# HGRN's values in a hybrid HGRN2 + RWKV-7 layer: turned by VectorE in 32x32 blocks and small transfers, where TensorE transposes did it

## The chip, the core and the metric

The kernel runs on one core of a Trainium2 chip. The metric is the time of one execution on the device in microseconds (us), and a version's time is the median of several runs. Engines are named as in the profile: PE is TensorE's matmul, PEld its weight load, DVE is VectorE, ACT is ScalarE, POOL is GpSimd, SP is SyncE, which here only issues transfers. Every engine works through its own instructions in a fixed order; an instruction that waits holds up all behind it.

## The reference, cut to what matters

One decoder layer over 2048 tokens of width 1024. A normalised input is projected once; four heads of HGRN2 and eight heads of RWKV-7 take their columns, their outputs are projected back, and a ConvFFN follows. The value `v` of this study is `i_raw`, of width 512, four heads of 128.

```python
h = _rmsnorm(x, norm1_w[l]);  proj = h @ w_in[l]
q_raw, f_raw, i_raw, g_raw = jnp.split(hg_p, 4, axis=-1)
...
f = lb + (1.0 - lb) * jax.nn.sigmoid(f_raw)
q = heads(jax.nn.silu(q_raw)) * (HG_HEAD_DIM ** -0.5);  k = heads(1.0 - f);  v = heads(i_raw)
# chunkwise: o_t = S_t^T q_t,  S_t = diag(f_t) S_{t-1} + k_t v_t^T
A = jnp.einsum('bhtk,bhsk,bhtsk->bhts', qb, kb, dec)
o = jnp.einsum('bhts,bhsv->bhtv', A, vb) + jnp.einsum('bhtk,bhkv->bhtv', qb * jnp.exp(b), S)
S = jnp.exp(b_last[:, :, 0, :])[..., None] * S + jnp.einsum('bhsk,bhsv->bhkv', kb * jnp.exp(b_last - b), vb)
```

The input projection yields `v` with channels on the 128 partitions and tokens along the row. The sums over `s` (tokens) on TensorE want tokens on the partitions: `v` has to be turned.

## The kernel before

The program has two stages. Stage one (`phase1`, up to about 1303 us) makes the projection, both mixers and most of the output projection; stage two the ConvFFN. The 2048 tokens are four blocks (`nb`) of 512. Stage one weaves three streams of work together:

- `dense`: per block 30 column groups of 128 (`P` jobs). Each is 24 matmuls `pj` (lines 270 to 272: high and low halves of inputs `hh`, `hl` and weights `wh`, `wl`) into one of two `pj` banks, and then an evacuation function takes the bank: `ev_rkv` and its kin for RWKV-7, `ev_q`, `ev_f`, `ev_v`, `ev_g` for HGRN. The four of HGRN's head `j` follow each other in this order. Between the blocks lie the transposes of the next input (`turn`), those of a finished block (job `N`: `transposed` with `to_h2`, tiles `h`, stored to `h2d`), and the output projection `out_block` (job `O`), which loads the mixers' output in tiles `oraw`.
- `rw_super`, eight times: RWKV-7 for a block and two pairs of heads. VectorE makes `M` (line 733) and block-turns `KB` to `KBb` (line 754); SP sends `KBb` on to `KBT` in 16 transfers (line 757), `M` to DRAM as `Ed` in four (line 745) and back as `E` in two (line 748). On `E`, VectorE runs a chain of 62 small steps (`etmp`, `Ti`, lines 802 and 804), then `TZ`, and PE goes on at line 821.
- `hg_unit`, 16 times: HGRN for a block and one head. Its first step turns `v`: four TensorE transposes (line 952) of the SBUF tile `hv` into a bank `hg`, and an ACT copy to `VT`. Then come scaled queries and keys `hX`, their matmuls (line 990), the turned keys `KT`, the products `KT` x `VT` (line 1055, the first user of `VT`) and `Af` x `VT` (line 1064).

Each round of the loop at the end of `phase1` takes one step (up to a `yield`) of `rw_super`, one of `hg_unit`, and 2000 ns by an estimate of `dense`. A scheduler then orders the instructions of each engine by its own model of their durations, so a change in one place moves others. Tiles named with a tag and `bufs=2` share two buffers in turn: tag `sg` holds the sigmoids `sgm` of `ev_q` and `ev_g` and, in `out_block`, `oraw`. SP's queue holds nearly all transfers but the weights, which POOL issues.

Of the kernel before, what the change touches and what calls it, by code (L numbers as in the profile page):

```python
# [7 lines left out]
F32 = mybir.dt.float32  # L8
# [3 lines left out]
AF = mybir.ActivationFunctionType  # L12
# [6 lines left out]
P = 128  # L19
# [48 lines left out]
def tile_layer(ctx, tc, consts, x, norm1_w, w_in, hg_lb_logits, hg_norm_w, rw_shift_mu, rw_w0, rw_w2,  # L68
# [4 lines left out]
    V, S, TE = nc.vector, nc.scalar, nc.tensor  # L73
    dma, store = nc.sync.dma_start, nc.gpsimd.dma_start
# [11 lines left out]
    ident = cp.tile([P, P], F32, name="ident")  # L86
# [27 lines left out]
    def act(out_, in_, func, **kw):  # L114

        want = tables.get(func)
        if want is not None and want != tab["now"]:
            pre = S.preload_act_table_set(want)
            for u_ in tab["uses"]:
                tc.add_manual_dep(pre.ins, u_.ins.name, NOSYNC, reason="table order")  # L120
            tab.update(now=want, pre=pre, uses=[])
        i_ = S.activation(out_, in_, func, **kw)  # L122
        if want is not None:
            tc.add_manual_dep(i_.ins, tab["pre"].ins.name, NOSYNC, reason="table order")
            tab["uses"].append(i_)
        return i_
# [119 lines left out]
    def split_to(hi, lo, src):  # L246
        c_ = S.copy(hi, src)
        return c_, V.tensor_sub(lo, src, hi.bitcast(F32))
# [25 lines left out]
    def phase1(c1):  # L274
# [3 lines left out]
        rp = c1.enter_context(tc.tile_pool(name="rp", bufs=1, reuse_waits="tile"))  # L278
# [18 lines left out]
        def bank(kind):  # L297
            return ps.tile([P, 512], F32, tag=kind, name=kind, bufs=2)
# [4 lines left out]
        stage = {}  # L303


        def stg(tag, name, bufs):
            return sp.tile([P, BLK], F32, tag=tag, name=name, bufs=bufs)
# [49 lines left out]

        def ev_v(nb, j):
            def f(acc):
                t_ = stg("hv", "hv", 2)  # L360
                act(t_, acc, AF.Copy)
                stage[("v", nb, j)] = t_
            return f

# [577 lines left out]


        def hg_unit(nb, j):
            q, f, v, gg = (stage.pop((n_, nb, j)) for n_ in "qfvg")
            k = rp.tile([P, BLK], F32, tag="hk", name="hk")
            V.tensor_scalar(k, f, -1.0, 1.0, ALU.mult, ALU.add)

            VT = rp.tile([P, 4, P], F32, tag="VT", name="VT")
            tp = bank("hg")  # L950
            for b in range(4):
                TE.transpose(tp[:, b * P:(b + 1) * P], v[:, b * P:(b + 1) * P], ident)
            act(VT, tp.rearrange("p (b t) -> p b t", t=P), AF.Copy)
            yield
            A = rp.tile([P, 4, 32], F32, tag="hA", name="A")
            Pf = f
            Sf = rp.tile([P, BLK], F32, tag="Sf", name="Sf")
# [83 lines left out]
            tp = bank("hg")  # L1041
# [12 lines left out]
            for b in range(4):  # L1054
                TE.matmul(sps[:, b * P:(b + 1) * P], KT[:, b, :], VT[:, b, :], start=True, stop=True)
            for b in range(4):
# [5 lines left out]
            for b in range(4):  # L1062
                ts_ = slice(b * P, (b + 1) * P)
                TE.matmul(op[:, ts_], VT[:, b, :], Af[:, b, :], start=True, stop=False)
                TE.matmul(op[:, ts_], SH[:, b, :], q[:, ts_], start=False, stop=True)
            sq = rp.tile([P, BLK], F32, tag="hk", name="osq")
            act(sq, op, AF.Square)
            hi, lo = (rp.tile([P, BLK], F32R, tag=tag, name="part") for tag in ("Sf", "VT"))
            split_to(hi, lo, sq)
# [22 lines left out]
        def hg_stream():  # L1092
            for n in range(4 * NBLK):
                while ready["hg"] <= n:
                    yield None
                yield from hg_unit(n // 4, n % 4)
# [47 lines left out]
    with ExitStack() as c2:  # L1144
# [36 lines left out]
        with tc.tile_pool(name="op", bufs=1, reuse_waits="tile") as op_:  # L1181
# [7 lines left out]
            b = NBLK - 1  # L1189
# [53 lines left out]
            for dh in range(2):  # L1243
                accs = [pst("wacc") for _ in range(4)]
                for n, k in enumerate((0, 1, 4, 5, 2, 3, 6, 7)):
# [16 lines left out]
                    if dh == 1 and 2 <= n:  # L1262
                        for j in range(2):
                            q = 2 * (n - 2) + j
# [3 lines left out]
                    for q in range(12):  # L1268
                        i, t_ = (q % 4, q // 4) if first else (q // 3, q % 3)
# [231 lines left out]
    with tc.tile_pool(name="dn", bufs=1, reuse_waits="tile") as dn:  # L1501
# [61 lines left out]
        for s_ in range(DS, N):  # L1563
            g, p, kk = steps[s_]
# [4 lines left out]
            acc = accs[DP[p][0]]  # L1569
# [55 lines left out]
```

## Time and profile before

| what | value |
|---|---|
| median of 3 runs | 2646.53 us (2640.78 to 2649.34) |
| the profiled execution, its own time | 2645.42 us |
| its span, first to last instruction | 2643.6 us |
| granted PE clock, mean | 0.994 |
| ACT copies `hv` and `VT` | 16 each, median 598 ns each |
| TensorE transposes of `hv` | 64 |
| transfers `KBb` to `KBT` | 128 of 64 KB |

The profile is of one execution. A row of a group gives how often an instruction ran, its busy time and the mean of one, then the idle time of its engine just before it and what ended it. Matmuls are pipelined, so that one starts before the last has ended: what one costs on PE is the distance from its start to the next one's, not its duration.

### The profile page before, as it was taken

Reading aid. Unit: us, or ns where it says so; the run is one execution under the profiler, and the core shown is the slowest. Engines: PE = TensorE matmul, PEld = TensorE weight load, DVE = VectorE, ACT = ScalarE, POOL = GpSimd, SP = SyncE. Lnnn points to the kernel's source line nnn. Section 1 sums busy time; section 2 is a strip of 40 time slices with the busy share of each in tenths; the row PEclk is TensorE's granted clock in tenths of the full one; section 3 lists DMA queues with packets and bytes.
Section 4 is the critical chain, followed back from the end, with each engine's and each line's share of the span. In section 5 each row is a group of like instructions: output and inputs, shape, how many; then the busy total and the mean of one; then the engine's idle time right before and its main releaser. Section 6 shows DMA issues by size and latency. Waiting matters only on the chain.

```text
span 2643.6 us, 51054 instructions
## 1 busy us (share of the span) xinstructions
PE 2547.0 (96%) x19467; PEld 2046.8 (77%) x19467; DVE 1963.7 (74%) x3744; ACT 1372.7 (52%) x2258; POOL 382.1 (14%) x686
## 2 busy tenths in 40 slices
PE   7999999999999999899899999999999999999998
PEld 5877777777777767777678888887888887888887
DVE  4868677676576765777678789988988887766556
ACT  5555444555545555344466654556554544545444
POOL 6433222212222122232100000000000000000000
PEclk9999999999999999999999999999999999999999
DMA  8846463555655565845583467747763553998655
GB/s 304 239 147 195 152 168 116 143 159 205 190 173 138 174 212 179 261 151 150 181 287 124 136 221 257 240 154 232 245 203 129 171 171 128 334 321 283 200 191 187
DMA packets 380298, 518.98 MB, mean 196 GB/s; under 512 B 114463, under 2 KB 211093, under 8 KB 380053
## 3 DMA queue, kind: packets, MB, share of 16 engines
q1 hardware_dynamic: 325521, 337.38, 40.1%
q0 software_dynamic: 54464, 178.32, 20.9%
q8 instruction: 153, 2.51, 0.4%
q14 instruction: 92, 0.75, 0.1%
q10 hardware_dynamic: 68, 0.02, 0.0%
HBM read 372.99 MB, written 134.22 MB: 192 GB/s over the span
## 4 chain that ended last, share of the span: by engine, by line
PE 70%; DVE 11%; ACT 8%; DMA 7%; issue 3%; POOL 0%; SPq 0%; DVEq 0%; ACTq 0%; POOLq 0%
PE pj L270 7%; PE pj L271 7%; PE pj L272 6%; PE ua L270 5%; PE ua L272 5%; PE ua L271 5%; PE da L271 3%; PE da L272 3%; PE da L270 3%; PE ud L271 2%; PE ud L270 2%; PE ud L272 2%; PE db L272 2%; PE db L271 2%; PE db L270 2%
## 5 line engine op out<-in xcount | busy, mean ns | idle before, releaser
L270 PE MATMUL pj<-hh,wh 128*128 128x512 f32 x960 | 391.6, 408 | 6.1 <-ACT rkv L122 4.0
L271 PE MATMUL pj<-hl,wh 128*128 128x512 f32 x960 | 377.4, 393 | 0.0
L272 PE MATMUL pj<-hh,wl 128*128 128x512 f32 x960 | 377.4, 393 | 0.0
L270 PE MATMUL ua<-Bh,uwh 128*128 128x512 f32 x704 | 276.4, 393 | 3.5 <-ACT m L122 2.2
L272 PE MATMUL ua<-Bh,uwl 128*128 128x512 f32 x704 | 274.3, 390 | 0.0
L271 PE MATMUL ua<-Bl,uwh 128*128 128x512 f32 x704 | 274.1, 389 | 0.0
L270 PEld LDWEIGHTS pj<-hh,wh 128*128 128x128 f32 x960 | 180.9, 189 | 54.5 <-issue 7.0
L272 PEld LDWEIGHTS pj<-hh,wl 128*128 128x128 f32 x960 | 180.8, 188 | 39.4 <-DMA wl<-Win171l 0.3
L271 PEld LDWEIGHTS pj<-hl,wh 128*128 128x128 f32 x960 | 181.0, 189 | 35.0 <-DVE hl L488 0.5
L254 ACT CAST uwh<-uraw 128x512 fp32r<-128x512 f32 x220 | 134.3, 617 | 135.0 <-PE ua L271 55.7
L255 DVE TENSOR_TENSOR dal<-draw,dah 128x512 fp32r<-128x512 f32 x138 | 95.2, 690 | 108.3 <-ACT dah L254 105.7
L255 DVE TENSOR_TENSOR uwl<-uraw,uwh 128x512 fp32r<-128x512 f32 x220 | 147.1, 684 | 34.3 <-ACT uwh L254 34.3
L254 ACT CAST dah<-draw 128x512 fp32r<-128x512 f32 x138 | 85.8, 621 | 160.0 <-PE da L271 75.5
L270 PEld LDWEIGHTS ua<-Bh,uwh 128*128 128x128 f32 x704 | 132.2, 188 | 33.9 <-ACT m L122 5.6
L272 PEld LDWEIGHTS ua<-Bh,uwl 128*128 128x128 f32 x704 | 132.2, 188 | 28.1 <-DVE uwl L255 0.4
L271 PEld LDWEIGHTS ua<-Bl,uwh 128*128 128x128 f32 x704 | 132.3, 188 | 26.7
L270 PE MATMUL ud<-Bh,uwh 128*128 128x512 f32 x352 | 138.0, 392 | 0.0
L1495 POOL DMA_DIRECT2D gd<-y x2 | 1.1, 542 | 943.1 <-DVE y L1493 943.1
L272 PE MATMUL ud<-Bh,uwl 128*128 128x512 f32 x352 | 137.1, 390 | 0.0
L271 PE MATMUL ud<-Bl,uwh 128*128 128x512 f32 x352 | 137.0, 389 | 0.0
L271 PE MATMUL da<-dbl,dah 128*128 128x512 f32 x332 | 129.4, 390 | 0.2 <-DVE dbl L255 0.2
L272 PE MATMUL da<-dbh,dal 128*128 128x512 f32 x332 | 129.2, 389 | 0.0
(582 smaller groups left out, 6203.0 us busy)
## 6 DMA issues: line engine op xcount, KB each, us to landing
uraw<-in_w_up_dram SPq DMA_DIRECT2D x176, 256.0 KB, 3.2
woraw<-in_w_out_dram POOLq DMA_DIRECT2D x96, 256.0 KB, 3.6
br<-gd SPq DMA_DIRECT2D x88, 256.0 KB, 4.3
draw<-Sg SPq DMA_DIRECT2D x88, 256.0 KB, 3.0
draw<-Tw SPq DMA_DIRECT2D x88, 256.0 KB, 3.9
gd<-y SPq DMA_DIRECT2D x86, 256.0 KB, 3.0
Sg<-br SPq DMA_DIRECT2D x72, 256.0 KB, 2.2
xt<-x1d SPq DMA_DIRECT2D x32, 512.0 KB, 6.5
```

The lines of the kernel that those rows point to most:

```text
L254: S.copy(hi, src)
L255: V.tensor_sub(lo, src, hi.bitcast(F32))
L270: TE.matmul(acc, lh, rh, start=first, stop=False, skip_group_check=skip)
L271: TE.matmul(acc, lh, rl, start=False, stop=False, skip_group_check=skip)
L272: TE.matmul(acc, ll, rh, start=False, stop=last, skip_group_check=skip)
L1495: (dma if end is None else nc.gpsimd.dma_start)(gd_[2 * h + b][fb * P:(fb + 1) * P, :], ys[0][:, b * BLK:(b + 1) * BLK])
```

## The change

`ev_v` no longer copies the bank to `hv` with ACT. VectorE reads the bank and turns each 32x32 block in its place into a tile `hvb`, which is taken from the `sg` buffers. Then SP issues 16 transfers from SBUF to SBUF, each 32 partitions by four pieces of 32 numbers (128 bytes), 16 KB in all, which put the blocks in their turned places in `hv`. `hv` is now what `VT` was. In `hg_unit` the four transposes, the bank they used, the ACT copy to `VT` and one `yield` are gone. The tag `VT` is still used for a part of the later sum of squares.

```diff
         def ev_v(nb, j):
             def f(acc):
-                t_ = stg("hv", "hv", 2)
-                act(t_, acc, AF.Copy)
+                t_ = stg("hv", "hv", 2).rearrange("p (b c) -> p b c", c=P)
+                y = stg("sg", "hvb", 2).rearrange("p (b a c) -> p b a c", a=4, c=32)
+                V.transpose(y.rearrange("p b a c -> p (b a c)"), acc)
+                for g in range(4):
+                    for a in range(4):
+                        dma(t_[32 * a:32 * a + 32, :, 32 * g:32 * g + 32], y[32 * g:32 * g + 32, :, a, :])
                 stage[("v", nb, j)] = t_
             return f
...
         def hg_unit(nb, j):
-            q, f, v, gg = (stage.pop((n_, nb, j)) for n_ in "qfvg")
+            q, f, VT, gg = (stage.pop((n_, nb, j)) for n_ in "qfvg")
...
-            VT = rp.tile([P, 4, P], F32, tag="VT", name="VT")
-            tp = bank("hg")
-            for b in range(4):
-                TE.transpose(tp[:, b * P:(b + 1) * P], v[:, b * P:(b + 1) * P], ident)
-            act(VT, tp.rearrange("p (b t) -> p b t", t=P), AF.Copy)
-            yield
```

Line numbers after `ev_v` grow by 4, those after the cut in `hg_unit` fall by 2. The scheduler's order changes with it. On SP, around the transfers of the second `rw_super`, there stood before:

```order
L1078 DMA oT_143<-osq 128x512
L757 DMA KBT<-KBb 32x16x32 x8
L745 DMA Ed<-M 32x16x32 x4
L757 DMA KBT<-KBb 32x16x32 x2
L748 DMA E<-Ed 64x1024 x2
L757 DMA KBT<-KBb 32x16x32 x6
```

and on SP at the same place there stands now:

```order
L761 DMA KBT<-KBb 32x16x32 x4
L365 DMA hv<-hvb 32x4x32 x16
L749 DMA Ed<-M 32x16x32 x4
L761 DMA KBT<-KBb 32x16x32 x2
L752 DMA E<-Ed 64x1024 x2
L761 DMA KBT<-KBb 32x16x32 x10
L365 DMA hv<-hvb 32x4x32 x16
```

A batch of 16 `hv` transfers now stands between the `KBT` transfers and `Ed`, and a second batch behind them.

On SP at the start of the first `out_block`, whose first loads are `oraw`, before:

```order
L748 DMA E<-Ed 64x1024 x2
L757 DMA KBT<-KBb 32x16x32 x6
L388 DMA oraw<-oT_143 128x512 x4
L403 DMA xh<-in_x_dram 128x512
L388 DMA oraw<-oT_143 128x512 x2
```

and on SP there now:

```order
L752 DMA E<-Ed 64x1024 x2
L761 DMA KBT<-KBb 32x16x32 x9
L365 DMA hv<-hvb 32x4x32 x16
L392 DMA oraw<-oT_143 128x512 x2
L1076 DMA oT_144<-osq 128x512
L392 DMA oraw<-oT_143 128x512 x3
```

The last `hv` batch of the block stands ahead of the first `oraw` load.

On PE at the first job `N` (the `pj<-ident,xt` rows are its transposes; the `rw<-AR,KB` rows are the matmuls whose results become `M`), before:

```order
L264 MATMUL pj<-ident,xt 128x128 x8
L952 MATMUL hg<-ident,hv 128x128 x4
L264 MATMUL pj<-ident,xt 128x128 x2
L730 MATMUL rw<-AR,KB 128x128 x16
L264 MATMUL pj<-ident,xt 128x128 x6
L730 MATMUL rw<-AR,KB 128x128 x2
L264 MATMUL pj<-ident,xt 128x128 x8
L730 MATMUL rw<-AR,KB 128x128 x2
L264 MATMUL pj<-ident,xt 128x128 x4
L730 MATMUL rw<-AR,KB 128x128 x12
L264 MATMUL pj<-ident,xt 128x128 x4
L270 MATMUL pj<-hh,wh 128x512
```

and on PE there now:

```order
L264 MATMUL pj<-ident,xt 128x128 x8
L734 MATMUL rw<-AR,KB 128x128 x2
L264 MATMUL pj<-ident,xt 128x128 x8
L734 MATMUL rw<-AR,KB 128x128 x12
L769 MATMUL rw<-ident,AR 128x128 x8
L988 MATMUL hg<-hq,hk 32x32 x16
L988 MATMUL hg<-hX 32x16 x15
L774 MATMUL rw<-cst,rkv_8132 128x128 x4
L264 MATMUL pj<-ident,xt 128x128 x4
L270 MATMUL pj<-hh,wh 128x512
```

The transposes of `hv` are gone, and other matmuls of both mixers have moved ahead of the last four transposes of the job.

## The prediction

> **What bounds the kernel now.** First the page's busy times, then the same by stage, cut where the ConvFFN begins.
>
> ```profile
> span 2643.6 us, 51054 instructions
> PE 2547.0 (96%) x19467; PEld 2046.8 (77%) x19467; DVE 1963.7 (74%) x3744; ACT 1372.7 (52%) x2258; POOL 382.1 (14%) x686
> ```
> ```profile
> 0.00:1303.00 1303.00, 1223.18 (x13629) 959.49 (x13630) 899.72 (x2138) 655.25 (x1102) 365.73 (x656) 0.99 0.59 182
> 1303.00:2643.00 1340.00, 1323.86 (x5840) 1087.32 (x5838) 1063.99 (x1606) 717.45 (x1157) 16.40 (x30) 1.00 0.64 211
> ```
>
> PE is busy for 1223 of 1303 us (94%) in stage one and 99% in stage two. The change lies wholly in stage one, whose order of work is bound by PE: DVE has 69% there, ACT 50%, the transfer engines 59%. What is left to PE as idle time is some 80 us in small pieces. The waits of PE in that stage show whose they are:
>
> ```profile
> PE rw L867 <- ACT M L122: 9.7, 6, 3.6
> PE pj L270 <- ACT hh L247: 6.0, 5, 2.0
> PE hg L1084 <- DVE part L248: 4.4, 7, 1.8
> PE rw L821 <- DVE TZ L808: 3.8, 4, 1.4
> PE pj L264 <- ACT hv L122: 0.6, 2, 0.3
> ```
>
> None is large, and the one that belongs to what goes (ACT's `hv`) is 0.6 us in total. So the gain has to be PE's own time, and a loss has to be a wait that grows.
>
> **The transposes that go.** PE's timeline at the first unit, and the group's row in the list by lines:
>
> ```profile
> 95.65 0.40 PE L272 MATMUL pj<-hh,wl 128*128 128x512 f32 x1
> 95.89 0.60 PE L952 MATMUL hg<-ident,hv 128*128 128x128 f32 x4
> 96.24 0.48 PE L270 MATMUL pj<-hh,wh 128*128 128x512 f32 x1
> ```
> ```profile
> L952 PE MATMUL hg<-ident,hv 128*128 128x128 f32 x64 | 10.7, 277 | 0.0
> ```
>
> From the start of the matmul before to the start of the one behind are 0.59 us; without the four transposes it would be the 0.23 us from 95.65 to 95.89 that a projection matmul takes. A group costs 0.36 us, 16 groups 5.8 us, all on the path: PE waited 0.0 us ahead of them, so no wait goes with them. By the row's durations it would be 64 x 277 ns = 17.7 us, but they overlap: four start within 0.35 us. I take 5.8.
>
> Skill against row: the Trainium skill, "VectorE: DVE Perf Modes", section The three transpose paths, gives a 128x128 transpose 390 ns on TensorE (for bf16) and 311 ns on VectorE; as an estimate, 64 of them would be 25.0 us and the time 2620. The trace disagrees: its group of four costs 0.36 us. The rules at the end of that page of the Trainium skill name TensorE for 128x128 and VectorE for blocks of 32x32 only, which speaks against this change; no row of this trace compares the two.
>
> **ACT and DVE.** The rows of the moved and the nearest similar work, by tile; the last is the landing of `KBT`'s transfers:
>
> ```profile
> L122 ACT ACTIVATE hv<-pj x16: 588/598/602, 84.3 to 1214.8; 128x512 f32<-128x512 f32 x16
> L122 ACT ACTIVATE VT<-hg x16: 578/598/601, 96.5 to 1238.8; 128x512 f32<-128x512 f32 x16
> L1055 PEld LDWEIGHTS hg<-VT,KT x128: 186/192/192, 126.5 to 1284.4; 128*128 128x128 f32 x128
> L754 DVE STREAM_TRANSPOSE KBb<-KB x16: 1192/1224/1243, 85.7 to 1184.9; 128x1024 f32<-128x1024 f32 x16
> L757 SPq DMA_DIRECT2D KBT<-KBb x128: 591/640/2658, 89.3 to 1205.6; - x128
> DMA to landing us min/median/max: 2.3/4.5/7.3
> ```
>
> ACT loses 32 copies of 0.598 us, 19.1 of its 655 us. It is off the path; the listed PE waits for ACT (9.7 + 6.0 + 0.6) would shrink by its share, 3%, 0.5 us. DVE gains 16 block transposes. The row of 1024 columns takes 1.22 us, so 512 take between half, 0.61, and all of it; I take 0.7 for half plus a start, 11 us in all, 1.2% of its 900. The listed PE waits for DVE (8.2 us) grow by 0.1. The bank is free when DVE has read it, where ACT did it before; the other `pj` bank carries 24 matmuls of 0.23 us, 5.4 us, so a bank may be late by about that before PE stops. ACT and DVE together: -0.5, and between -2 and +2 if the waits react more strongly.
>
> **The 16 transfers per unit, 256 in all.** The turned values are due late: the first `hv` was copied at 84.3 and first used by PE at 126.5, so 42 us cover the detour. What costs is the place in SP's queue and in the buffers. The price of one issue is not in the trace. These SP rows bound it:
>
> ```profile
> 101.93 15.27 SPq L757 DMA_DIRECT2D KBT<-KBb  x10
> 144.40 0.34 SPq L1078 DMA_DIRECT2D oT<-osq  x1
> 228.72 6.98 SPq L757 DMA_DIRECT2D KBT<-KBb  x8
> 238.43 3.29 SPq L745 DMA_DIRECT2D Ed<-M  x4
> 241.76 1.60 SPq L757 DMA_DIRECT2D KBT<-KBb  x2
> 246.69 1.15 SPq L748 DMA_DIRECT2D E<-Ed  x2
> ```
>
> An `hv` transfer has 32 x 4 = 128 pieces. A `KBT` transfer has 512 pieces of the same 128 bytes and takes 0.64 us; a store of `oT` has 128 larger pieces and takes 0.34. I take 0.34, nearest by the number of pieces: a batch of 16 is 5.4 us, at `KBT`'s pace 10.2 us, and at the pace of the slowest run (15.27 / 10 = 1.53) 24.4 us.
>
> Behind the batch wait `Ed`, `E`, and with them DVE's chain. The second `rw_super`, where the batch now stands right ahead of `Ed`, on ACT and DVE, and the landing of all `E` transfers:
>
> ```profile
> 233.53 0.59 ACT L122 ACTIVATE hv<-pj 128x512 f32<-128x512 f32 x1
> 249.93 0.60 ACT L122 ACTIVATE sgm<-pj 128x512 f32<-128x512 f32 x1
> ```
> ```profile
> 235.92 2.48 DVE L733 TENSOR_TENSOR M<-rw,cst 128x512 f32<-128x512 f32 x4
> 253.94 0.18 DVE L802 TENSOR_TENSOR etmp<-E,Ti 128x31 f32<-128x31 f32 x1
> ```
> ```profile
> DMA to landing us min/median/max: 3.5/4.6/5.6
> ```
>
> `M` was done at 238.4 and `Ed` went at 238.43; `E` was issued by 247.8 and landed, with its 4.6 us, at 252.4, and DVE took it at 253.9: 1.5 us to spare. Now the block transpose is done near 234.2 and the batch near 239.6, so `Ed` is 1.2 us late, covered. At 0.64 us it ends at 244.4, 6.0 us late, 4.5 past the cover, and DVE would stand still with everything behind it, the evacuations too. Such a place is met in about four of the eight supers, as `hv` comes twice per super and the other batch lies behind `E`. Ends: 0 and 4 x 4.5 = 18 us; I take 1.
>
> Buffers: the next `ev_q` writes its sigmoid over `hvb`, at 249.9. The batch has landed by 239.6 + 4.5 = 244.1, or 248.9 at `KBT`'s pace: covered both times. At the output projection the first `oraw` inherits `hvb`'s buffer:
>
> ```profile
> 529.64 28.24 SPq L388 DMA_DIRECT2D oraw<-oT  x4
> ```
> ```profile
> oraw<-oT SPq DMA_DIRECT2D x20, 256.0 KB, 2.7
> ```
> ```profile
> 540.64 0.60 ACT L122 ACTIVATE hv<-pj 128x512 f32<-128x512 f32 x1 [4.84 <-PE pj L272]
> 552.01 0.62 ACT L247 CAST hh<-oraw 128x512 fp32r<-128x512 f32 x1
> ```
>
> The first load, issued at 529.6 before, now waits for the last batch: 541.3 + 5.4 + 2.3 (least landing of such pieces) = 549.0, and with 2.7 us for its own way (the median of the 20 such loads) 551.7, just in time for 552.0. At 0.64 us it is 4.8 us late, and so in the second `out_block`. Ends 0 and 9.6; I take 0.5.
>
> The transfer engines get 32,768 more packets of 128 bytes, 4 MB on 519; at 59% share that stays beside.
>
> **The order at job `N`.** Here the store of a tile `h` frees the buffer of a later one:
>
> ```profile
> 710.21 1.32 ACT L122 ACTIVATE h<-pj,vt 128x512 f32<-128x512 f32 x2 [2.19 <-DMA h2d<-h]
> ```
> ```profile
> 710.95 0.50 PE L270 MATMUL pj<-hh,wh 128*128 128x512 f32 x1 [0.68 <-ACT h L122]
> ```
>
> Seven of the eight `h2d` stores now stand behind an `hv` batch of 5.4 us (10.2 at the upper price). ACT waits longer there, but PE has been given 43 other matmuls ahead of the last transposes, so PE's 0.68 us may vanish or grow to the batch's excess, about 5. Two such places: -1.4 to +10; I take 0.
>
> **Sum.** -5.8 - 0.5 + 1 + 0.5 + 0 = -4.8 us. The profiled execution took 2645.4 us (span 2643.6 and 1.8 around it); its own sum is 2640.6. That execution is 1.1 us under the median of the three runs, which is well within their spread of 8.6, so I forecast 2640.6, 0.2% under the median. A measurement of this kernel can tell about 0.3%, 8 us, from no change.
>
> **Rivals.**
> First, faster by more than that: the scheduler's new order also closes PE gaps (job `N`, -1.4; ACT's shorter queue, -2; one bank `hg` less per unit). -5.8 - 2 - 1.4 = -9.2, 2636.2. For it: 80 us of idle PE lie in small pieces; against it: no wait named after `hv` or `VT` is above 0.6 us. Chance 0.31.
> Second, the gain is given back: the first `oraw` is late in two blocks and a part of the four `Ed` too, 6 us over the forecast, 2646.6. For it: the covers are 0.3 and 1.5 us. Chance 0.20.
> Third, slower, by one mechanism: issues at `KBT`'s 0.64 us or slower, `Ed` behind the batch. +18 - 5.8 = +12.2, 2657.6; at 1.53 us the batch ends 20 us late and it is far more. It decides from about 0.6 us per issue, where four supers lose 14 us together. For it: slow runs like the 15.27 us do occur; against it: the piece count. Chance 0.13. The Trainium skill, "DMA: Bandwidth & Descriptors", section Rules for kernel authors, says that transfers under 64 KB are mostly overhead and should be joined; these are 16 KB, and the queue's rows bear it out as issue time alone.
> Fourth, the transposes held PE for their full 17.7 us: 2627.7. The overlap in the timeline speaks against it. Chance 0.02.
>
> **How the numbers follow.** The forecast itself has 0.34, and its own range, 2637 to 2644, dips a little into "faster". Faster: 0.31 + 0.02 + 0.04 = 0.37; same: 0.30 + 0.20 = 0.50; slower 0.13. The range reaches from a bit below the first rival to short of the third, 2630 to 2654; what lies outside is most of the third rival and the fourth.
>
> **What would show it.** PE's rows of 128x128 transposes of `hv` gone and stage one some 5 us shorter with the same stage two; `hv` issues near 0.34 us each in SP's timeline; the first `etmp` of each super without DVE idle time naming `E`; no ACT wait of `sgm` for `hv`; the first `hh` of the output projection no later. Wrong it would be if the waits of DVE for `E`, or of ACT for `oraw` and `h2d`, carry more than about 5 us in sum, or if the new order shifts waits that have nothing to do with `v`.

## The result and the profile after

The change made the kernel slower: median 2683.18 us (2676.00 to 2686.21, 4 runs) against 2647.25 us for the kernel before beside it, ratio 1.0132, 95% interval 1.0112 to 1.0153. The forecast was 2640.6 us, with 2630 to 2654 as its range.

The first rows of the page after, and the windows cut at the same places. A window's row gives its length, the busy time of PE, PEld, DVE, ACT and POOL with the number of instructions, then the granted PE clock, the share of the transfer engines and GB/s:

```profile
span 2680.7 us, 51271 instructions
PE 2563.5 (96%) x19403; PEld 2052.1 (77%) x19403; DVE 1980.2 (74%) x3760; ACT 1370.1 (51%) x2236; POOL 381.1 (14%) x686
```
```profile
0.00:1303.00 1303.00, 1211.59 (x13412) 943.33 (x13412) 902.00 (x2124) 639.76 (x1057) 359.90 (x647) 0.98 0.60 181
1303.00:2680.00 1377.00, 1351.92 (x5992) 1108.82 (x5992) 1078.19 (x1637) 730.37 (x1179) 21.16 (x39) 1.00 0.63 209
```

No engine has become the bound. In the first 1303 us PE is busy 11.6 us less (1223.18 before), with 217 fewer matmul records, of which the transposes that went are 64: it is behind. The first matmul of the ConvFFN's up projection starts at 1392.0 us, against 1359.2 before (from 1303 to there PE mostly does the rest of the output projection): 32.8 of the 37.1 us of longer span arise ahead of the ConvFFN's matmuls, where the change lies.

The new instructions, by tile: the transfers on SP's queue, and VectorE's block transpose.

```profile
L365 SPq DMA_DIRECT2D hv<-hvb x256: 585/599/1845, 86.4 to 1258.1; - x128
```
```profile
L362 DVE STREAM_TRANSPOSE hvb<-pj x16: 705/713/717, 85.6 to 1246.6; 128x512 f32<-128x512 f32 x16
```

The transpose takes the 0.7 us assumed. An issue holds SP for 0.599 us (median), not 0.34. SP's queue at the second `rw_super`, the place shown before:

```profile
236.85 3.01 SPq L761 DMA_DIRECT2D KBT<-KBb  x4
242.15 10.77 SPq L365 DMA_DIRECT2D hv<-hvb  x16
253.02 2.14 SPq L749 DMA_DIRECT2D Ed<-M  x4
255.20 1.29 SPq L761 DMA_DIRECT2D KBT<-KBb  x2
256.92 1.47 SPq L752 DMA_DIRECT2D E<-Ed  x2
```
```profile
244.42 2.48 DVE L737 TENSOR_TENSOR M<-rw,cst 128x512 f32<-128x512 f32 x4
```

VectorE finished `M` at 246.9; `Ed` went at 253.0, 6.1 us late, behind a batch of 10.8 us. Before, it went at once. A batch stands ahead of `Ed` in all eight supers, not in four, and `Ed` was 1.7 to 8.2 us late. What VectorE, ScalarE and PE wait for in stage one, after:

```profile
DVE hk L951 <- DMA oT<-osq: 11.5, 5, 4.1
DVE etmp L806 <- DMA E<-Ed: 7.9, 4, 5.8
```
```profile
ACT h L122 <- DMA h2d<-h: 5.2, 2, 2.8
ACT hh L247 <- DMA oraw<-oT: 7.5, 7, 2.3
```
```profile
PE pj L270 <- ACT hh L247: 10.9, 8, 2.5
PE hg L1042 <- DVE hk L1035: 7.4, 5, 3.5
PE pj L264 <- ACT h L122: 6.2, 4, 2.3
```

The wait for `E` had no row before; those for the `oT` store, `h2d` and `oraw` were:

```profile
DVE hk L947 <- DMA oT<-osq: 3.0, 2, 2.1
```
```profile
ACT hh L247 <- DMA oraw<-oT: 11.9, 9, 3.6
ACT h L122 <- DMA h2d<-h: 2.2, 1, 2.2
```

So three of the four grew, and the one for `oraw` shrank. These small waits don't add up to 36 us by themselves, and the program after has another order than the one before, so a row-by-row comparison is no proof. The experiments had to take the order out.

### The profile page after: what moved, and what is told of

Same layout as the page of the kernel before. It is cut to its first block, busy times and chain, and to the rows that moved or that the text cites. A ratio compares the mean times of both kernels' runs of the same rounds, so it can differ in the third digit from the quotient of the medians.

```text
span 2680.7 us, 51271 instructions
## 1 busy us (share of the span) xinstructions
PE 2563.5 (96%) x19403; PEld 2052.1 (77%) x19403; DVE 1980.2 (74%) x3760; ACT 1370.1 (51%) x2236; POOL 381.1 (14%) x686
## 4 chain that ended last, share of the span: by engine, by line
PE 61%; DVE 12%; DMA 8%; ACT 6%; issue 5%; SPq 2%; POOL 0%; DVEq 0%; ACTq 0%; POOLq 0%
PE pj L270 5%; PE ua L270 5%; PE pj L272 5%; PE ua L272 5%; PE ua L271 5%; PE pj L271 5%; PE da L271 2%; PE da L272 2%; PE ud L271 2%; PE ud L270 2%; PE ud L272 2%; PE da L270 2%; PE db L270 2%; PE db L271 2%; PE db L272 2%
```

## The experiments

Every ratio is to the kernel before, timed beside it on the same chip. "Unread" transfers write to a tile that nothing reads; runs without transfers leave the values turned in blocks only; "pinned" is explained further down. Medians in different rows can come from different chips, so where two rows are compared the ratios are the safer numbers.

| run | median us | ratio, 95% interval |
|---|---|---|
| changed, no transfers | 2653.06 | 1.0037 (1.0022 to 1.0051) |
| before + 16 unread transfers per unit | 2676.67 | 1.0123 (1.0099 to 1.0147) |
| changed, transfers behind `E` | 2689.53 | 1.0171 (1.0144 to 1.0198) |
| changed, own buffer for `hvb` | 2675.16 | 1.0117 (1.0088 to 1.0146) |
| changed, five transfers by way of DRAM | 2669.80 | 1.0084 (1.0059 to 1.0109) |
| before, one step less per unit | 2668.36 | 1.0078 (1.0051 to 1.0106) |
| changed, step kept | 2678.32 | 1.0116 (1.0086 to 1.0146) |
| changed, transfers on POOL's queue | 2681.34 | 1.0134 (1.0113 to 1.0154) |
| before, `TICK` 1950 / 2050 | 2646.92 / 2659.05 | 1.0009 (0.9997 to 1.0020) / 1.0054 (1.0037 to 1.0071) |
| changed, no transfers, step kept | 2646.00 | 1.0002 (0.9987 to 1.0016) |
| changed, five transfers, step kept | 2659.70 | 1.0064 (1.0039 to 1.0089) |
| pinned: transfers, in the order without | 2698.38 | 1.0194 (1.0172 to 1.0217) |
| pinned: before + 16, in the order of before | 2693.07 | 1.0176 (1.0156 to 1.0196) |
| pinned: no transfers, in the order with | 2646.94 | 0.9999 (0.9987 to 1.0011) |
| pinned: before, in the order with 16 | 2658.45 | 1.0052 (1.0031 to 1.0072) |
| pinned: before + 16 of a quarter | 2687.18 | 1.0161 (1.0130 to 1.0193) |
| pinned: before + 8 | 2657.37 | 1.0046 (1.0027 to 1.0065) |

**Which part of the change: the transfers.** One run takes them out of the changed kernel, one adds them to the kernel before.

```diff
-                y = stg("sg", "hvb", 2)...
-                V.transpose(y..., acc)
-                for g in range(4):
-                    for a in range(4):
-                        dma(t_[...], y[...])
+                V.transpose(t_.rearrange("p b c -> p (b c)"), acc)
```

> The changed kernel with the 16 transfers per unit left out: VectorE turns the 32x32 blocks straight into hv, and the blocks are not put in their turned places, so the values are wrong in order; all else as in the changed kernel. Queue theory (a batch of 16 issues of 0.6 us stands on SP ahead of Ed, E and oraw): the loss goes with the transfers, 2638 to 2644 us. Buffer theory (hvb in the sg buffers holds up sigmoids and oraw): the same, as hvb is gone too. Order theory (one step fewer per unit, the scheduler's new order): stays at 2675 to 2690. VectorE theory (the bank is emptied by the busier engine): stays at 2670 to 2690.

```diff
                 act(t_, acc, AF.Copy)
+                z = stg("sg", "hz", 2).rearrange("p (b c) -> p b c", c=P)
+                y = t_.rearrange("p (b a c) -> p b a c", a=4, c=32)
+                for g in range(4):
+                    for a in range(4):
+                        dma(z[32 * a:32 * a + 32, :, 32 * g:32 * g + 32], y[32 * g:32 * g + 32, :, a, :])
```

> The kernel before, with its TensorE transposes, plus the same 16 transfers per unit on SP from hv to a tile in the sg buffers that nothing reads. Queue theory: 36 us for the change and 6 for the transposes that stay, 2675 to 2695 us. Buffer theory: the same. Order theory and VectorE theory: 2645 to 2652, as neither has changed.

Without them the changed kernel takes 2653.06 us, 30 less than with (25 by the ratios); with them the kernel before takes 2676.67, 34 more than its own 2643.02. The transfers are most of the loss, though nobody reads them in the second run. Some 10 us remain without them.

**By which way: three places for them.** The first two runs issue them elsewhere (the first from `hg_unit`, with a buffer of its own for `hvb` and another tag for one tile `part`); the third takes `hvb` from buffers that the sigmoids don't use.

```diff
+                    i_ = dma(VT[...], hvb[...])                    # in hg_unit
+                    tc.add_manual_dep(i_.ins, last_E[0].ins.name, NOSYNC, reason="after E")
```

> The changed kernel with all 256 transfers on SP at the same pace, but issued from hg_unit and only behind the two E transfers of the rw_super at hand; hvb has a buffer of its own. Queue theory with the wait for Ed as its core: 2640 to 2655 us. Buffer theory: 2640 to 2655. If the sheer number of issues or of packets costs the time: 2670 to 2690. Order theory and VectorE theory: 2670 to 2690.

```diff
-                        dma(t_[...], y[...])
+                        nc.gpsimd.dma_start(t_[...], y[...])
```

> The changed kernel with the 16 transfers issued by POOL, whose queue holds the weights, in place of SP. Queue theory: SP's Ed, E, oraw, h2d and oT are on time again, 30 us back, 2650 to 2660 us, less what the weights behind the batch on POOL lose (up to 15). Packet theory: no change, 2675 to 2690.

```diff
-                y = stg("sg", "hvb", 2)...
+                y = rp.tile([P, BLK], F32, tag="VT", name="hvb")...
```

> The changed kernel with hvb in the buffer of tag VT in place of the sg buffers; the transfers stand where they stood. Buffer theory: 2640 to 2655 us. Queue theory: 2670 to 2685, a little gained at the two output projections whose first oraw no longer waits for the batch. Order and VectorE theories: 2670 to 2690.

None helps by more than 8 us, and each of the two moves finds another victim. Behind `E` the batches of two units stand in one row (32 transfers, 35.3 us, in the first super), in front of the stores of `osq` (23.4 us of VectorE's waits, 3.0 before). On POOL's queue, where one issue takes 0.549 us, it is the weights (25.0 us of ScalarE's waits for `wraw`, 6.7 before). So the theory "only `Ed` behind the batch", which I held after the first look, was too narrow. The waits, behind `E` and on POOL:

```profile
DVE hk L949 <- DMA oT<-osq: 23.4, 7, 8.3
```
```profile
L365 POOL DMA_DIRECT2D hv<-hvb x256: 549/549/647, 87.8 to 1258.7; - x128
```
```profile
ACT wh L254 <- DMA wraw<-in_w_in_dram: 25.0, 5, 9.2
```

The buffer run's 8 us less (4 by the ratios) is a difference between overlapping intervals.

**Fewer issues.**

```diff
-                for g in range(4):
-                    for a in range(4):
-                        dma(t_[...], y[...])
+                Vd = dp.tile([4, 32, 4, 4, 32], F32, tag="Vd", name="Vd", bufs=2)
+                for g in range(4):
+                    dma(Vd[:, :, :, g, :].rearrange("a r b c -> r b a c"), y[32 * g:32 * g + 32])
+                dma(t_, Vd.rearrange("a r b g c -> (a r) b (g c)"))
```

> The changed kernel with five transfers per unit in place of 16: four put the 32-partition slices of hvb into a DRAM tile in turned order, one reads it back whole; the same sg buffer. The batch on SP is then about 2.5 us in place of 9.6. Queue theory (what stands behind the batch on SP comes late, 30 us in all for 256 issues): 2654 to 2662 us. Packet theory (32,768 small packets slow all transfers): 2675 to 2690, as the small packets stay. Order theory for the 10 us that were lost without any transfer: they stay here, so not below 2650.

2669.80 us: 13 less than the change, although all the small pieces are still moved, and then read again. By the medians of its rows the five issues are 2.9 us per unit in place of 9.6:

```profile
L365 SPq DMA_DIRECT2D Vd<-hvb x64: 570/630/2795, 84.0 to 1242.5; - x64
L366 SPq DMA_DIRECT2D hv<-Vd x16: 320/344/1189, 98.3 to 1248.7; - x16
```

**The step that went with the transposes.** Without the `yield` that the change took out of `hg_unit`, each unit has one step fewer, and so 2 us of `dense` work less (by the program's estimate) between the mixers' steps. The first run takes that `yield` alone out of the kernel before; the second puts it back into the changed one.

```diff
-            yield
```

> The kernel before, only the yield behind the transposes of hg_unit removed, so that each unit has one step fewer; transposes and ACT copies stay, no transfers. Order theory for the 16 us between the 10 lost without transfers and the 6 gained by the transposes: 2655 to 2663 us. VectorE theory (emptying the bank by VectorE costs it): 2640 to 2648.

> The changed kernel with a yield at the place of the one removed, so that each unit has as many steps as before. Order theory: 16 us back, 2660 to 2670 us. VectorE theory: 2677 to 2690.

Together with the runs below it costs 21 us in the kernel before (its ratio, 1.0078), 7 without transfers (2653.06 to 2646.00), 10 with five (2669.80 to 2659.70) and 5 with sixteen (2683.18 to 2678.32; these last two pairs have overlapping intervals). It is a part of the loss that the forecast had no term for.

At this point I suspected the order itself, because these sizes differ so much and every variant also showed more stretches of halved PE clock (7 before, 10 to 18 in the variants). Four runs were to test it: one number of the kernel before changed, and two variants with the step kept.

```diff
-TICK = 2000.0
+TICK = 1950.0
```

> The kernel before, with one number changed: TICK, the amount of dense PE work that the program writes between two steps of the recurrences, is 1950 ns and not 2000. No instruction is added or taken away; only the order in which they are written shifts a little. Theory of the order (the order before is one in which few gaps of PE reach a full clock window, and any shift brings back some): slower by 5 to 20 us, about 2655, with more than the seven half-clock windows of before, ten to thirteen. Theory of the transfers alone (everything that the change lost is issue time and waits in the transfer queue): no transfers are added here, so it stays within 5 us of before, with six to eight half-clock windows.

> The same in the other direction: the kernel before with TICK at 2050 ns. Theory of the order: slower by 5 to 20 us, whichever way the number is moved. A plain effect of the amount of dense work per step (the step that the change takes out of each unit is 2 us of dense work less) would be of opposite signs at 1950 and 2050: one slower, one faster by about the same. Theory of the transfers alone: within 5 us of before.

> The changed kernel without the 16 transfers per unit (the values then stand transposed in blocks only, so this part of the turn is left out), VectorE writing straight into hv, and with the step of the scheduler put back that the change took out of each unit. What is left of the change is VectorE's block transpose for the TensorE transposes and the two copies of ScalarE. If the first experiment's +10 us was the lost step, this gives the 5.8 us of the prediction: 2638 to 2644, at or under before. If it was VectorE's extra work or the general sensitivity to the order, it stays 5 to 15 us above before, about 2655.

> The changed kernel with five transfers per unit by way of DRAM in place of 16, and the step put back. Theory that queue time and lost step add up: 2669.8 less what the step is worth (21 us when it was taken from the kernel before, 5 when it was put back into the changed one), 2650 to 2665. Theory of the order as a draw: no gain that can be foreseen, 2655 to 2685.

Shifting the order moves the time by 2 us (an interval that includes no change) and by 14; so order matters, but less than the transfers. With the step kept and no transfers the changed kernel is level with the kernel before (1.0002): VectorE's turn in place of PE's brings nothing that can be measured. So a version with the whole turn that beats the kernel before isn't to be expected along this way: the one without its transfers doesn't, and the best with the whole turn, the one with five, takes 2659.70.

**Order or queue: two squares.** With 256 transfers in the program the scheduler writes 2,800 to 3,100 of 14,600 PE instructions in other places. To separate the two, the order of PE, VectorE, ScalarE and POOL was pinned from a table taken from the other program; SP's queue was left free.

```diff
         tile_layer(tc, *args)
+        pin(tc, nc)
...
+        for d in struct.unpack(f"<{len(raw) // 2}h", raw):
+            at += 1 + d
+            i = by[e][at]
+            if last is not None:
+                tc.add_manual_dep(i, last.name, NOSYNC, reason="order")
+            last = i
```

> The changed kernel with its step kept, all 256 transfers in it, but TensorE, VectorE, ScalarE and GpSimd run their instructions in exactly the order that the scheduler wrote for the program without transfers (the one that took 2646.0 us). Theory of the order: the 32 us between 2646.0 and 2678.3 come from the other order, so this returns to 2646 to 2656. Theory of the queue and the waits: they come from 9.6 us of issue per batch in front of Ed, KBT, oraw and h2d, and in an order that makes no room for it the waits are no smaller: 2675 or above.

> The kernel before with 256 transfers added that nobody reads (2676.7 us when the scheduler was free), TensorE, VectorE, ScalarE and GpSimd pinned to the order of the kernel before. Theory of the order: 2644 to 2655. Theory of the queue and the waits: 2670 or above.

> The changed kernel with its step kept and without its transfers (the values then stand transposed in blocks only: this part of the turn is left out), pinned to the order that the scheduler wrote for the program with the transfers. Theory of the order: slow although no transfer is left, 2665 to 2680. Theory of the queue and the waits: back to 2646 to 2655, since nothing stands in the queue any more.

> The kernel before, no instruction added, pinned to the order that the scheduler wrote when the 256 unread transfers were in the program. Theory of the order: 2665 to 2680. Theory of the queue and the waits: within 10 us of before, 2644 to 2654.

| changed kernel, step kept | order without | order with |
|---|---|---|
| no transfers | 2646.00 | 2646.94 |
| 16 transfers per unit | 2698.38 | 2678.32 |

| kernel before | its own order | order with 16 |
|---|---|---|
| as it is | 2647.99 | 2658.45 |
| + 16 unread transfers | 2693.07 | 2676.67 |

My theory of the order falls as the cause of the loss. In a fixed order the transfers cost 52 us (2646.00 to 2698.38) and 31 in the other; the other order costs 1 us by itself in the one program and 10 in the other. Without transfers the pinned program is level with the kernel before (0.9999), so the pinning itself costs nothing that can be measured. The scheduler, far from doing the harm, took back 20 and 16 us of it.

The pair in the order without transfers can be read instruction by instruction. SP's queue and VectorE's first `etmp` in the first super, without:

```profile
91.54 2.83 SPq L757 DMA_DIRECT2D KBT<-KBb  x3
95.14 3.14 SPq L745 DMA_DIRECT2D Ed<-M  x4
98.32 1.29 SPq L757 DMA_DIRECT2D KBT<-KBb  x2
101.60 1.15 SPq L748 DMA_DIRECT2D E<-Ed  x2
```
```profile
109.44 0.19 DVE L802 TENSOR_TENSOR etmp<-E,Ti 128x31 f32<-128x31 f32 x1 [0.57 <-DMA E<-Ed]
```

and with the transfers:

```profile
84.92 12.21 SPq L365 DMA_DIRECT2D hv<-hvb  x16
97.24 1.29 SPq L761 DMA_DIRECT2D KBT<-KBb  x2
98.62 4.81 SPq L749 DMA_DIRECT2D Ed<-M  x4
103.48 2.59 SPq L761 DMA_DIRECT2D KBT<-KBb  x2
108.39 1.15 SPq L752 DMA_DIRECT2D E<-Ed  x2
```
```profile
115.99 0.19 DVE L806 TENSOR_TENSOR etmp<-E,Ti 128x31 f32<-128x31 f32 x1 [7.98 <-DMA E<-Ed]
```

The batch holds the queue until 97.1, `E` goes 6.8 us later, and VectorE stands for 7.98 us. The same kernel's waits of VectorE and ScalarE for what SP's queue brings, over stage one:

```profile
DVE etmp L806 <- DMA E<-Ed: 25.7, 5, 8.0
```
```profile
ACT UV L122 <- DMA KBT<-KBb: 20.5, 3, 11.4
ACT h L122 <- DMA h2d<-h: 14.6, 2, 7.3
ACT hh L247 <- DMA oraw<-oT: 14.3, 8, 4.7
```

In the same order without transfers these are 2.9 us, 1.1, no row, and 10.2:

```profile
DVE etmp L802 <- DMA E<-Ed: 2.9, 2, 2.3
```
```profile
ACT hh L247 <- DMA oraw<-oT: 10.2, 7, 2.7
ACT UV L122 <- DMA KBT<-KBb: 1.1, 1, 1.1
```

The four together grow by 60.9 us, against 52 us of time; not every wait of VectorE and ScalarE reaches PE. PE's own lag (the start of each of the 3456 projection matmuls of lines 270 to 272 with the transfers, less its start without) rises to 49.9 us over stage one, and seven steps make 39 of them, each at a place where the trace names what was late:

| lag step of PE, us | at, us (with) | late there |
|---|---|---|
| +5.2 | 122 | `E`, first super (wait 8.0) |
| +3.1 | 422 | `E` (2.9) |
| +4.2 | 578 | `oraw`, first `out_block` (4.7) |
| +6.5 | 743 | `h2d` store, job `N` (7.2) |
| +5.9 | 799 | an input tile `xt` for ScalarE (5.0) |
| +7.7 | 928 | `KBT` (11.4) |
| +6.6 | 1104 | `h2d` store, second job `N` (7.3) |

**What about the transfers: issues or packets.** Both in the order of the kernel before, with transfers that nobody reads.

```diff
-                        dma(z[..., :, 32 * g:32 * g + 32], y[32 * g:32 * g + 32, :, a, :])
+                        dma(z[..., 0, 32 * g:32 * g + 32], y[32 * g:32 * g + 32, 0, a, :])
```

> The kernel before, its order pinned, with 16 unread transfers per unit as in the run of 2693.1 us, but each moves one block of 32x32 values and not four: 32 packets of 128 bytes in place of 128. Theory of the queue (the issue holds SP for about 0.6 us whatever it moves): nearly the full price, 2680 to 2693, with an issue row at 0.55 to 0.6 us. Theory of the traffic (packets crowd the transfer engines): the price falls to about a quarter of the 45 us, 2652 to 2662, and E and KBT land sooner.

```diff
-                    for a in range(4):
+                    for a in range(2):
```

> The kernel before, its order pinned, with 8 unread transfers of full size per unit in place of 16: half the issues and half the packets. Theory of the queue: a batch holds SP for 4.8 us and not 9.6, so a place loses what is left over its cover; the three etmp places with 4 to 8 us of loss at 16 fall to 0 to 3, in all less than half the price, 2650 to 2665. If the price were the same for every transfer, half of 45 us, about 2670.

The issue rows by tile, of a quarter's size and of half the number:

```profile
L366 SPq DMA_DIRECT2D hz<-hv x256: 507/589/1797, 83.9 to 1268.2; - x128
```
```profile
L366 SPq DMA_DIRECT2D hz<-hv x128: 585/600/1594, 85.6 to 1233.8; - x128
```

With a quarter of the packets an issue still takes 0.589 us, and the kernel is 44 us over the kernel before beside it (2643.14), as with whole ones (45): nearly all of the price is that of the issues. The two intervals (1.0130 to 1.0193 and 1.0156 to 1.0196) leave room for a few microseconds that are the packets'. With half the issues at full size it falls to 2657.37, 14 us over, and not half of 45: where what waits behind a batch has some microseconds to spare, the first half of the batch is nearly free. This run also keeps the buffer that the batch takes from the sigmoids, so that buffer costs 14 us at most here. VectorE's wait for `E` in the run of 8 issues, of 16 quarters, and of 16 whole transfers:

```profile
DVE etmp L807 <- DMA E<-Ed: 0.9, 2, 0.6
```
```profile
DVE etmp L807 <- DMA E<-Ed: 9.5, 4, 5.0
```
```profile
DVE etmp L807 <- DMA E<-Ed: 14.1, 6, 5.0
```

With a quarter of the packets the wait for `E` is shorter, though the time is not by more than the noise.

The Trainium skill, "DMA: Bandwidth & Descriptors", section Rules for kernel authors, says that issuing from several engines gains no bandwidth and saves only issue time. Here issue time was nearly the whole cost, and moving it to POOL still saved nothing (1.0134 against 1.0132): there the weights waited behind it.

## Why the prediction was wrong, point by point

- **The issue price is the step that failed.** I took 0.34 us, from the `oT` store, "nearest by the number of pieces". Measured: 0.599 us, and 0.589 with a quarter of the pieces. The number of pieces is not what sets it. The nearer row was `KBT`'s 0.64 us, which is also a transfer within SBUF over 32 partitions and stood in the prediction as the upper bound. What part of that likeness matters is open: from 32 partitions to DRAM, in 512 pieces of the same size, `Ed` took 0.494 us in the kernel before and `Vd` 0.630 in the five-transfer run.
- **The ends were not independent.** `Ed` (0 to 18), `oraw` (0 to 9.6) and job `N` (up to +10) all hung on that one price. At 0.64 us they come together: 2645.4 - 5.8 - 0.5 + 18 + 9.6 + 10 = 2676.7, against 2683.18 measured. That this comes near is in part luck, as the next points show: the terms were mis-sized both ways. Only the third rival had the price, for `Ed` alone: 2657.6 with a chance of 0.13, and already outside the range. That rival had the right mechanism and the right sign, and a third of the size (12 of 36 us).
- **The terms, in a fixed order**: `E` 22.8 us of new waits (end given 18), job `N`'s `h2d` 14.6 (10), `oraw` 4.1 (9.6), and `KBT` 19.4, for which there was no term: I had listed `Ed` and `E` as waiting behind the batch, but not the other transfers of the same chain. In the changed kernel itself, in its own order, the wait for the `oT` store grew most (8.5 us) and had no term either, while the one for `oraw` shrank by 4.4.
- **The 1.5 us to spare for `Ed`** were read off one super, and "about four of the eight" was too few: a batch stands ahead of `Ed` in all eight, at other distances. VectorE stood longest in the first super, 8 us in the fixed order and 5.8 in the changed kernel; in the fixed order without transfers it already waited 0.57 us for `E` there, so nothing was to spare.
- **The removed step** (`yield`) was named among the edits but got no term; 5 to 10 us in the changed kernel's variants.
- **The transposes that go, -5.8, and -0.5 for ACT and DVE.** The run with the turn alone is at 1.0002 (0.9987 to 1.0016), -3.4 to +4.2 us, which excludes -6.3 for that program in its own order. PE's work is less, and the time is not. Whether VectorE's longer evacuations, PE's shorter runs or the new order gave it back isn't settled.
- **Right**: 0.7 us for the block transpose; no wait of a sigmoid for `hvb`; most of it in stage one (4.3 of the 37.1 us of longer span lie behind it); and the statement of what would show an error: the waits for `E` and `h2d` come to 13.1 us, against 2.2 before, and with `oraw` to 20.6 against 14.1.
- **Slips in the working**, which change nothing above: at 0.64 us the first `oraw` would be 4.5 us late and not 4.8 (9.0 for two blocks), at 0.6 us four supers lose 15.5 us and not 14, and the list of PE's waits leaves out the longest, 11.1 us for a constant at the program's start.

The sum as measured, from the runs with one thing changed at a time, each in the scheduler's own order: turn alone about 0, transfers +32 (2646.00 to 2678.32), step +5 (2678.32 to 2683.18): 37 on 2646, which is 2683.

## What to carry to other kernels

Count a queue's issues, not its bytes: here sixteen small transfers were 10 us in which nothing else of that queue started, so list every later user of the queue with its slack, place by place. When several terms of an estimate share one unknown price, move them together to get the range. And when a scheduler rewrites the order, pin it to the other version's order before blaming it; here that took the wrong culprit out of the case.

## What was not expected of the hardware

- The issue of a transfer within SBUF over 32 partitions takes 0.59 to 0.64 us on SP for 32, 128 or 512 pieces of 128 bytes; the store of `oT`, with 128 larger pieces over 128 partitions, 0.34, and the read of 128 partitions from DRAM in the five-transfer run 0.344. From POOL the transfer of 128 pieces took 0.549. These are medians; a single `KBT` issue of the kernel before took 2.66 us.
- PE's granted clock halves in stretches of one to three times 3.4 us, right behind a stretch of 3.4 us in which PE was busy for 0.14 to 0.73 of the time (the 14 stretches of the changed kernel ahead of the ConvFFN's matmuls). In the first super after the change VectorE waits for `E` until 115.5, its chain is late, PE waits 3.5 us for the `hk` behind it, and then runs at half clock:

```profile
115.52 0.19 DVE L806 TENSOR_TENSOR etmp<-E,Ti 128x31 f32<-128x31 f32 x1 [5.77 <-DMA E<-Ed]
```
```profile
PE hg L1042 <- DVE hk L1035: 3.5, 1, 3.5
```
```profile
124.30:127.70 3.40, 0.67 (x5) 0.53 (x6) 3.40 (x12) 2.18 (x7) 1.16 (x2) 0.97 0.93 282
127.70:131.10 3.40, 3.40 (x14) 2.81 (x15) 2.12 (x7) 0.97 (x2) 1.29 (x2) 0.53 0.76 237
```

In these windows PE is busy for 0.67 us of 3.4, and then has a clock of 0.53. The Trainium skill, "TensorE: Matmul & The Clock Gate", Part 1, gives half clock after an idle window of about 3.4 us. The trace agrees in the length and in the half clock, but in none of these 14 was PE idle for the whole window ahead. Summed from the trace's clock records, such stretches take 34.4 us before and 77.1 after, and up to the ConvFFN's first up projection 41.0 (without transfers) and 88.7 (with) in the fixed order. So a wait that empties PE can be paid for again behind it: as an estimate, 47.7 us more at half clock cost PE 23.9 us at most, of the 52. How much of the loss is this part was not tried by itself: the two runs without transfers and with the step kept had 41.0 and 44.4 us of such stretches there, against 27.3 before, at no loss of time.
